# A Trainium2 backbone kernel: paired heads in the attention's values, summed filter weights, the inverses' block copies on other engines, and the products for L behind the DeltaNet preparation

## The chip, the core and the metric

The kernel runs on one core of a Trainium2 chip. The metric is the device time in microseconds of one execution, as the median of several runs. A core has TensorE (PE, matrix products, with PEld for its weight loads), VectorE (DVE), ScalarE (ACT), GpSimd (POOL) and SyncE (SP). In this kernel SyncE issues the transfers. Each engine takes its instructions in a fixed order.

## What is computed

One inference step of a hybrid backbone: two layers, width 1024, over 128 context tokens and 512 latent tokens, which the kernel holds side by side as 640 columns. Layer 0 is a half-step SwiGLU FFN, then RWKV-7 time mixing with 8 heads of 64 beside a gated DeltaNet with 4 heads of 128, then a second half-step FFN. Layer 1 has latent attention (8 heads) beside a Hyena convolution of order 2 in the same place. Every sub-layer is normalised and modulated by the condition.

The parts of the reference that the change meets:

```
def wkv7_scan(r, w, k, v, kk, a, S0):
    def step(S, xs):
        r_t, w_t, k_t, v_t, kk_t, a_t = xs
        sk = jnp.einsum('bhvk,bhk->bhv', S, kk_t)
        S = (S * w_t[:, :, None, :] - sk[..., None] * (kk_t * a_t)[:, :, None, :]
             + v_t[..., None] * k_t[:, :, None, :])
        return S, jnp.einsum('bhvk,bhk->bhv', S, r_t)
...
def gated_delta_chunked(q, k, v, g, beta, S0):
...
    T = lax.linalg.triangular_solve(eye + lower, jnp.broadcast_to(eye, lower.shape),
                                    left_side=True, lower=True, unit_diagonal=True)
...
def mla_attend(q_nope, q_pe, k_nope, k_pe, v):
...
        s = jnp.einsum('bqhd,bkhd->bhqk', qn, k_nope) + jnp.einsum('bqhr,bkr->bhqk', qp, k_pe)
        prob = jax.nn.softmax(s.astype(jnp.float32) * scale, axis=-1).astype(v.dtype)
        return jnp.einsum('bhqk,bkhd->bqhd', prob, v)
...
def hyena_filters(L, w1, b1, w2, b2, w3, freq):
...
    h = jnp.sin(freq[0] * (feats @ w1 + b1))
    h = jnp.sin(freq[1] * (h @ w2 + b2))
    h = (h @ w3).reshape(L, D_ORDER, 2, D_WIDTH)
...
    return h * window[:, None, None, :].astype(h.dtype)

def bidir_fftconv(z, h_f, h_b):
...
    filt2 = jnp.concatenate([h_f, jnp.zeros((1, C), h_f.dtype), h_b[:0:-1]], axis=0).astype(jnp.float32)
```

The final states and the compressed caches are returned besides the two outputs.

## The kernel before

Activations lie with channels on the 128 partitions and the 640 tokens along the free axis, in two halves of 320 columns. Large products are made of three: an activation and a weight are each split into a high and a low part (`hh` and `hl`, `wh` and `wl`), and high by high, low by high and high by low are summed in PSUM. The weights' split is a cast on ScalarE (`L470`, `L654`) and a subtraction on VectorE or GpSimd (`L471`, `L655`). All matmuls go through the helper `mm`, so most of TensorE's rows in the profile have its line, L287, and are told apart by the names of their tiles.

The order of instructions on each engine comes from the tile framework: it is given a program in the order of the Python code, simulates it with its own costs, and puts each engine's instructions in the order that this gives. An edit in one place can therefore move instructions in another. Pools with a number of buffers per name (`w` has 8, `PT` 2, `iv` 4) make a tile wait until the one that had its buffer is no longer read.

The stages, with their times in the profiled execution: the Hyena filters and the first modulations (0 to 93 us), the first FFN (to about 540), the input projection of layer 0 with the preparation of head pairs 0 and 1 (to about 895), the chunked scans with the preparation of pairs 2 and 3 (to about 1300), the output projection, two FFNs (to 2317), the latents (to 2390), the attention's heads with the Hyena convolution (to 2685), the output projection, and the last FFN from about 2750.

Four places matter here.

`filters()` makes the convolution filters. Two small layers with sines give features of 64 channels, doubled on both halves of the partitions; `hw3` holds the third layer's weights for both orders o and both directions d. For each order and each of five blocks of 128 tokens, two products (forward, backward) are multiplied by the window on VectorE (`fa`, `fb`), then GpSimd adds and subtracts them into `hpl` and `hmi`. For the first two blocks the backward filter's first token is zeroed (`nz`). Then `hpl` and `hmi` are transformed (`dfp`, `dfw`).

`rwkv_prep()` makes the scaled keys and queries of one pair of RWKV heads (tiles `w`, `kd`), and at its end the lower triangular blocks `L`: 40 products of 64 by 64 and four multiplications by a mask (L1116). Behind these comes the bonus term `b2`. `gdn_prep()` makes the same kind of blocks, `LT`, for one DeltaNet head. `prepare(i)` calls both, and then `inverses()`.

`inverses()` inverts 32 by 32 triangular blocks of both: they are stored to DRAM and loaded so that 120 blocks lie on 120 partitions (`iv`); 20 of them need a transpose, done by four strided copies on ScalarE (L1155). Then rows are eliminated one after the other (`invert_blocks`, L824 and L826), 8 of the 32 columns on GpSimd (`X0`), 24 on VectorE (`X8`). The results are stored, and four strided copies on ScalarE (L1168) make their transposes, which are stored too. Both come back with 28 loads or so on SyncE's queue (L1176 to L1182), and other stores and loads, those of the projection among them (`pd`, L871; `wr`, L469), stand in the same queue.

In the projection, a strip's PSUM is evicted into `pp` (L749 to L751), shifted against its neighbours (L881 with L882, or L911 with L912 and L913), put through an activation (L870) and stored to `pd`.

`heads()` runs over 8 heads and five blocks of 128 queries. `values()` transposes the probabilities into `PT`, and at a head's last block makes five products with `V` that write 64 rows of a PSUM bank: the lower rows for even heads, the upper for odd ones. ScalarE copies these into `om` (L1772), and after each odd head `om` is stored.

## Time and profile before

| | us |
|---|---|
| runs | 3216.09, 3218.57, 3236.96 |
| median of the runs | 3218.57 |
| profiled execution | 3213.42 |
| its span | 3211.6 |

The span is the time from the first to the last instruction of the profiled execution. The rows of the profile name a line, an engine, an operation, and the tiles written and read. In grouped rows the number behind the bar is busy time, then the mean duration in nanoseconds, then the idle time of the engine just before the group and what ended most of it. Stretches are given in microseconds from the span's start.

### The profile page before, as it was taken

The page shows a single profiled execution, that of the slowest core. Times are in us where ns is not written, and L with a number is a line of the kernel's source. Part 1 is how long each engine was busy: PE and PEld are TensorE (multiplying, and loading weights), DVE is VectorE, ACT ScalarE, POOL GpSimd, SP SyncE. Part 2 cuts the span into 40 slices and gives each one's busy share as a digit, 9 for nine tenths or more (in the row PEclk, how much of TensorE's full clock was granted, in tenths as well). Part 3 has the DMA queues.
Part 4 walks back from the last instruction along what each step waited for, and adds up shares of the span by engine and source line. Part 5 has one row for each costly group of instructions (what it writes and reads, how often), then busy time and mean ns, then how long its engine had stood idle before and what let it go on. Part 6 is the DMA issues. An engine that isn't in the chain of part 4 may idle for free.

```text
span 3211.6 us, 56035 instructions
## 1 busy us (share of the span) xinstructions
PE 2995.3 (93%) x21505; PEld 2680.3 (83%) x21505; DVE 2254.6 (70%) x3995; ACT 1375.1 (43%) x2876; POOL 1206.8 (38%) x1110
## 2 busy tenths in 40 slices
PE   7899999998789999889999979999999998899998
PEld 2799999987766666879999979999888747899998
DVE  5956667568678755695666797777865686877777
ACT  2523334566466644442333453333544423533333
POOL 4733334226425300273333474444310021644442
PEclk9999999999888988899999989999999999899999
DMA  7464542456465322445553222222421215222222
GB/s 267 148 205 162 180 135 72 168 167 170 126 155 128 84 75 66 144 145 187 170 172 121 83 93 90 84 79 83 128 61 51 85 50 180 66 86 82 87 83 82
DMA packets 277587, 385.36 MB, mean 120 GB/s; under 512 B 128704, under 2 KB 161120, under 8 KB 275400
## 3 DMA queue, kind: packets, MB, share of 16 engines
q1 hardware_dynamic: 277160, 381.13, 37.6%
q8 instruction: 169, 2.77, 0.3%
q14 instruction: 98, 0.80, 0.1%
q0 software_dynamic: 160, 0.66, 0.1%
HBM read 330.29 MB, written 51.42 MB: 119 GB/s over the span
## 4 chain that ended last, share of the span: by engine, by line
PE 53%; DVE 13%; DMA 4%; ACT 4%; issue 3%; POOL 1%; SPq 1%; DVEq 0%; ACTq 0%; POOLq 0%
PE ps L287 52%; DMA wr<-in_wd_dram 1%; DVE wl L655 1%; DMA wr<-in_wo_dram 1%; DVE nx L539 1%; DVE inv L824 1%; DVE wl L471 1%; DVE X L826 1%; DVE nacc L514 0%; PE ps L1765 0%; DMA pd<-o 0%; DVE b L605 0%; POOL X L826 0%; ACT wh L470 0%; DVE nx L710 0%
## 5 line engine op out<-in xcount | busy, mean ns | idle before, releaser
L287 PE MATMUL ps<-hh,wh 128*128 128x320 f32 x2208 | 694.7, 316 | 21.1 <-ACT pp L750 13.3
L287 PE MATMUL ps<-hl,wh 128*128 128x320 f32 x2208 | 690.2, 314 | 3.0 <-POOL hl L546 2.7
L287 PE MATMUL ps<-hh,wl 128*128 128x320 f32 x2208 | 681.1, 313 | 8.8 <-DVE wl L471 4.6
L287 PE MATMUL ps<-b,wh 128*128 128x320 f32 x2112 | 480.8, 315 | 36.0 <-DVE b L605 20.1
L287 PEld LDWEIGHTS ps<-hh,wh 128*128 128x128 f32 x2208 | 419.6, 190 | 36.4 <-ACT pp L750 13.6
L287 PEld LDWEIGHTS ps<-hh,wl 128*128 128x128 f32 x2208 | 417.3, 190 | 12.1 <-DVE wl L471 5.6
L287 PEld LDWEIGHTS ps<-hl,wh 128*128 128x128 f32 x2208 | 419.6, 190 | 7.3 <-POOL hl L546 3.9
L287 PEld LDWEIGHTS ps<-b,wh 128*128 128x128 f32 x2112 | 360.9, 192 | 43.9 <-DVE b L605 22.3
L287 PE MATMUL ps<-hidl,wh 128*128 128x320 f32 x1248 | 383.2, 309 | 0.0
L287 PE MATMUL ps<-hidh,wh 128*128 128x320 f32 x1248 | 382.6, 312 | 0.0
L287 PE MATMUL ps<-hidh,wl 128*128 128x320 f32 x1248 | 381.0, 309 | 0.9 <-DVE wl L471 0.9
L550 DVE SCALAR_TENSOR_TENSOR x<-ps,mod,x 128x128 f32<-128x128 f32 (+2 forms) x528 | 212.3, 434 | 215.7 <-PE ps L287 214.2
L655 POOL TENSOR_TENSOR wl<-S,wh 128x512 fp32r<-128x512 f32 x176 | 253.1, 1438 | 280.8 <-ACT wh L654 279.2
L684 POOL TENSOR_TENSOR S<-wr,wu 128x512 f32<-128x512 f32 x88 | 131.7, 1497 | 587.7 <-DMA wr<-in_wgu_dram 366.9
L287 PE MATMUL ps<-b,wl 128*128 128x320 f32 x1056 | 329.8, 314 | 10.4 <-DVE wl L655 7.8
L470 ACT CAST wh<-wr 128x512 fp32r<-128x512 f32 (+2 forms) x210 | 157.8, 754 | 394.0 <-PE ps L287 307.9
L654 ACT CAST wh<-S 128x512 fp32r<-128x512 f32 (+1 forms) x264 | 201.2, 764 | 241.8 <-PE ps L287 186.6
L471 DVE TENSOR_TENSOR wl<-wr,wh 128x512 fp32r<-128x512 f32 (+2 forms) x210 | 187.0, 893 | 86.2 <-ACT wh L470 84.2
L287 PEld LDWEIGHTS ps<-hidh,wh 128*128 128x128 f32 x1248 | 232.7, 188 | 13.2 <-issue 7.4
L287 PEld LDWEIGHTS ps<-hidh,wl 128*128 128x128 f32 x1248 | 233.3, 188 | 1.2 <-DVE wl L471 1.2
L287 PEld LDWEIGHTS ps<-hidl,wh 128*128 128x128 f32 x1248 | 233.9, 188 | 0.0
L287 PEld LDWEIGHTS ps<-b,wl 128*128 128x128 f32 x1056 | 202.2, 192 | 13.2 <-DVE wl L655 9.8
(455 smaller groups left out, 6047.9 us busy)
## 6 DMA issues: line engine op xcount, KB each, us to landing
wmod<-in_wmod_dram SPq DMA_DIRECT2D x288, 256.0 KB
wr<-in_wgu_dram SPq DMA_DIRECT2D x108, 512.0 KB
wu<-in_wgu_dram SPq DMA_DIRECT2D x88, 512.0 KB
wr<-in_wd_dram SPq DMA_DIRECT2D x80, 320.0 KB
wr<-in_wd_dram SPq DMA_DIRECT2D x96, 256.0 KB
pd<-o SPq DMA_DIRECT2D x32, 320.0 KB
wr<-in_abg_dram SPq DMA_DIRECT2D x17, 512.0 KB
wr<-in_wo_dram SPq DMA_DIRECT2D x16, 512.0 KB
```

The source lines that it names most:

```text
L287: self.nc.tensor.matmul(out=out, lhsT=lhsT, rhs=rhs, start=start, stop=stop)
L470: nc.scalar.copy(out=wh, in_=w)
L471: nc.vector.tensor_sub(out=wl, in0=w, in1=wh.bitcast(F32))
L539: nc.vector.scalar_tensor_tensor(out=xn[:, a:b], in0=self.x[c][:, k, a:b], scalar=A, in1=r[:, a:b], op0=ALU.mult, op1=ALU.mult)
L550: self.nc.vector.scalar_tensor_tensor(out=self.x[c][:, d, a:b], in0=q[:, a:b], scalar=gate[:, cond, d:d + 1], in1=self.x[c][:, d, a:b], op ...
L654: nc.scalar.copy(out=hi, in_=r)
L655: eng.tensor_tensor(out=lo, in0=r, in1=f32(hi), op=ALU.subtract)
L684: G.tensor_tensor(out=out, in0=x, in1=y, op=op)
L824: eng.tensor_tensor(out=tm, in0=L[s // 16][:, s % 16, t].unsqueeze(1).broadcast_to([np_, a, b]), in1=X[:, :a, s].unsqueeze(2).broadcast_to ...
L826: eng.tensor_tensor(out=X[:, :a, t], in0=X[:, :a, t], in1=tm, op=ALU.subtract)
```

## The change

Four edits:

1. In `values()`, nothing is multiplied at an even head's end. At an odd head's end ten products follow one another, the even head's and the odd head's in turn, into the lower and the upper 64 rows of one bank, and one copy of 128 rows evicts both.
2. In `filters()`, the forward and backward weights are replaced by their sum and their difference before the products, so that a product times the window is already `hpl` or `hmi`. The adds on GpSimd go. Where the backward filter's first token has to be zero, row 0 of both results is set to half of their sum. The blocks are taken in the order (0, 3), (1, 4), (2), in which neighbours read the lower and the upper 64 partitions.
3. In `inverses()`, the four transposing copies at the beginning go to GpSimd, and those at the end to the engine that made the columns: GpSimd for `X0`, VectorE for `X8`.
4. In `rwkv_prep()`, the products and masks for `L` are wrapped in `late()`, which `prepare()` calls behind `gdn_prep()`.

```diff
@@ -936,6 +936,7 @@
                 self.gdn_gates()
             self.mark(f"gA{i}")
             G[i] = self.gdn_prep(i, sets[i % 3])
+            R[i]["late"]()
             self.mark(f"J{i}")
             if i > 0:
                 next(inv[i - 1])
@@ -1100,21 +1101,23 @@
         for d, (kd, G) in enumerate(ks):
             nc.vector.tensor_mul(out=kd, in0=kd, in1=G)
             put(XD, d, d, kd)
-
-        at, _ = CONST["rmask"]
-        mask = self.const[:, at:at + CH].unsqueeze(1)
-        n = NCH // 2
-        for c0 in range(0, NCH, n):
-            qs = [self.ps("ma"), self.ps("ma")]
-            for i in range(n):
-                for d in range(2):
-                    for hh, q in enumerate(qs):
-                        hr = slice(64 * hh, 64 * hh + 64)
-                        self.mm(q[64 * d:64 * d + 64, CH * i:CH * i + CH], PQ[d][1][hr, c0 + i], PQ[d][0][hr, c0 + i])
-            for hh, q in enumerate(qs):
-                g = NCH * hh + c0
-                nc.vector.tensor_tensor(out=L[:, g:g + n], in0=q[:, :n * CH].rearrange("p (u m) -> p u m", u=n),
-                                        in1=mask.broadcast_to([P, n, CH]), op=ALU.mult)
+        def late():
+
+            at, _ = CONST["rmask"]
+            mask = self.const[:, at:at + CH].unsqueeze(1)
+            n = NCH // 2
+            for c0 in range(0, NCH, n):
+                qs = [self.ps("ma"), self.ps("ma")]
+                for i in range(n):
+                    for d in range(2):
+                        for hh, q in enumerate(qs):
+                            hr = slice(64 * hh, 64 * hh + 64)
+                            self.mm(q[64 * d:64 * d + 64, CH * i:CH * i + CH], PQ[d][1][hr, c0 + i], PQ[d][0][hr, c0 + i])
+                for hh, q in enumerate(qs):
+                    g = NCH * hh + c0
+                    nc.vector.tensor_tensor(out=L[:, g:g + n], in0=q[:, :n * CH].rearrange("p (u m) -> p u m", u=n),
+                                            in1=mask.broadcast_to([P, n, CH]), op=ALU.mult)
+
 
         nc.vector.scalar_tensor_tensor(out=kds, in0=kds, scalar=self.col("r_k", hp), in1=r, op0=ALU.mult, op1=ALU.mult)
         q = self.both(blk, kds, "ma")
@@ -1124,7 +1127,7 @@
             nc.vector.scalar_tensor_tensor(out=b2[:, cs], in0=q[c][:, :H], scalar=0.5, in1=v[:, cs], op0=ALU.mult, op1=ALU.mult)
         b2d = self.t(self.dp, [P, T], "b2", bufs=4)
         nc.sync.dma_start(out=b2d, in_=b2)
-        return dict(ZD=ZD, XD=XD, L=L, eG=eG, b2=b2d)
+        return dict(ZD=ZD, XD=XD, L=L, eG=eG, b2=b2d, late=late)
 
 
     def inverses(self, R, G):
@@ -1152,7 +1155,7 @@
             nc.sync.dma_start(out=raw[i], in_=dr[0][:g0, 16 * i:16 * i + 16])
         for i in range(2):
             for j in range(2):
-                nc.scalar.copy(out=L[i][:g0, :, 16 * j:16 * j + 16], in_=raw[j].rearrange("p t s -> p s t")[:, 16 * i:16 * i + 16])
+                nc.gpsimd.tensor_copy(out=L[i][:g0, :, 16 * j:16 * j + 16], in_=raw[j].rearrange("p t s -> p s t")[:, 16 * i:16 * i + 16])
         xs = []
         for j0, nj, eng in ((0, NPOOL, nc.gpsimd), (NPOOL, 32 - NPOOL, nc.vector)):
             X = self.t(ra, [nb, nj, 32], f"X{j0}")
@@ -1161,11 +1164,11 @@
             nc.gpsimd.memset(flat[:, j0::33], 1.0)
             self.invert_blocks(eng, L, X, j0, self.t(ra, [nb, 192], "inv", bufs=2))
             nc.sync.dma_start(out=dr[1][:, j0:j0 + nj], in_=X)
-            xs.append((X, j0))
+            xs.append((X, j0, eng))
         for i in range(2):
             xt = iv([nb, 16, 32])
-            for X, j0 in xs:
-                nc.scalar.copy(out=xt[:, :, j0:j0 + X.shape[1]], in_=X.rearrange("p s t -> p t s")[:, 16 * i:16 * i + 16])
+            for X, j0, eng in xs:
+                eng.tensor_copy(out=xt[:, :, j0:j0 + X.shape[1]], in_=X.rearrange("p s t -> p t s")[:, 16 * i:16 * i + 16])
             nc.sync.dma_start(out=dr[2][:, 16 * i:16 * i + 16], in_=xt)
         yield
 
@@ -1765,13 +1768,14 @@
                     nc.tensor.transpose(out=q[:, P * i:P * i + P], in_=pr[:, P * (g + i):P * (g + i) + P], identity=ident)
                 nc.vector.tensor_copy(out=PT[hh][:, g:g + n, P * (qi - 1):P * qi],
                                       in_=q[:, :P * n].rearrange("p (k t) -> p k t", k=n))
-            if qi == 4:
+            if qi == 4 and e == 1:
+
                 q = self.ps("tr")
                 for i in range(5):
-                    self.mm(q[rows], V[:, 1 + i, 64 * hh:64 * hh + 64], PT[hh][:, i], start=i == 0, stop=i == 4)
-                nc.scalar.copy(out=om[hh // 2][rows, P:], in_=q[rows])
-                if e == 1:
-                    nc.sync.dma_start(out=mix[hh // 2], in_=om[hh // 2])
+                    for g in (hh - 1, hh):
+                        self.mm(q[64 * (g % 2):64 * (g % 2) + 64], V[:, 1 + i, 64 * g:64 * g + 64], PT[g][:, i], start=i == 0, stop=i == 4)
+                nc.scalar.copy(out=om[hh // 2][:, P:], in_=q)
+                nc.sync.dma_start(out=mix[hh // 2], in_=om[hh // 2])
 
         units = [(hh, qi) for hh in range(8) for qi in range(5)]
         project(0)
@@ -1838,20 +1842,26 @@
         hb = self.t(fp, [P, 2, 512], "hbias")
         nc.sync.dma_start(out=hb, in_=I["hbias"].unsqueeze(0).broadcast_to([P, 2, 512]))
         for o in range(2):
+
+            w0, w1 = [W["hw3"][:, (2 * o + d) * 512:(2 * o + d) * 512 + 512] for d in range(2)]
+            nc.vector.tensor_tensor(out=w0, in0=w0, in1=w1, op=ALU.add)
+            nc.vector.scalar_tensor_tensor(out=w1, in0=w1, scalar=-2.0, in1=w0, op0=ALU.mult, op1=ALU.add)
             hpm = [self.t(fp, [P, 5, 512], n) for n in ("hpl", "hmi")]
-            for t in range(5):
-                q = [self.ps("mx"), self.ps("mx")]
-                for d in range(2):
-                    r, c = (slice(0, 64), t) if t < 3 else (slice(64, P), t - 3)
-                    self.mm(q[d], x[r, P * c:P * c + P], W["hw3"][r, (2 * o + d) * 512:(2 * o + d) * 512 + 512])
-                a, b = self.t(fp, [P, 512], "fa", bufs=2), self.t(fp, [P, 512], "fb", bufs=2)
-                nc.vector.tensor_tensor(out=a, in0=q[0], in1=W["win"][:, t], op=ALU.mult)
-                if t < 2:
-                    nc.vector.scalar_tensor_tensor(out=b, in0=q[1], scalar=self.con("nz"), in1=W["win"][:, t], op0=ALU.mult, op1=ALU.mult)
-                else:
-                    nc.vector.tensor_tensor(out=b, in0=q[1], in1=W["win"][:, t], op=ALU.mult)
-                nc.gpsimd.tensor_tensor(out=hpm[0][:, t], in0=a, in1=b, op=ALU.add)
-                nc.gpsimd.tensor_tensor(out=hpm[1][:, t], in0=a, in1=b, op=ALU.subtract)
+
+            for ts in ((0, 3), (1, 4), (2,)):
+                q = {(t, d): self.ps("mx") for t in ts for d in range(2)}
+                for d, w in enumerate((w0, w1)):
+                    for t in ts:
+                        r, c = (slice(0, 64), t) if t < 3 else (slice(64, P), t - 3)
+                        self.mm(q[t, d], x[r, P * c:P * c + P], w[r])
+                for t in ts:
+                    for d in range(2):
+                        nc.vector.tensor_tensor(out=hpm[d][:, t], in0=q[t, d], in1=W["win"][:, t], op=ALU.mult)
+                    if t < 2:
+                        a, b = hpm[0][0:1, t], hpm[1][0:1, t]
+                        nc.vector.tensor_tensor(out=a, in0=a, in1=b, op=ALU.add)
+                        nc.scalar.mul(out=a, in_=a, mul=0.5)
+                        nc.scalar.copy(out=b, in_=a)
                 yield
             bias = hb[:, o]
             for cs in range(2):
```

What this makes of the order, at three places. In these rows the number behind a name is the tile's, and the two programs count tiles apart.

TensorE at the end of the first head, before. `PT` are its probabilities, `ch` and `cl` the latents that the next heads' keys are made of:

```order
L287 MATMUL ps_26233<-hh_25346,wl_26228 128x320
L287 MATMUL ps_26311<-ch_25499,wh_26302 128x384
L287 MATMUL ps_26063<-PT_25961,V_25776 64x512 x5
L1912 MATMUL ps_26142<-const_58,cv_26135 128x128 x4
L287 MATMUL ps_26311<-cl_25500,wh_26302 128x384
L287 MATMUL ps_26311<-ch_25499,wl_26303 128x384
```

And at the first place of this kind after the change, at the end of the second head:

```order
L287 MATMUL ps_26697<-ql_25452,wh_26690 128x320
L287 MATMUL ps_26697<-qh_25451,wl_26691 128x320
L287 MATMUL ps_26451<-PT_25937,V_25752 64x512
L287 MATMUL ps_26451<-PT_26349,V_25752 64x512
L287 MATMUL ps_26451<-PT_25937,V_25752 64x512
L287 MATMUL ps_26451<-PT_26349,V_25752 64x512
```

The products stand at the end of every second head, and the rows of the first and the second head (`PT_25937`, `PT_26349`) take turns, ten in all; before, five of one head stood together.

ScalarE in the projection, where pair 1's inverses begin, before. `iv` and `zg` are blocks of pair 0's and pair 1's inverses, `o` the shifted strips, `wh` a weight's high part:

```order
L1195 ACTIVATE iv_8105<-ps_8107 32x320 x2
L1195 ACTIVATE iv_8105<-ps_8108 32x320 x2
L1201 ACTIVATE zg_8106<-ps_8109 128x160
L911 ACTIVATE o_8721<-pp_1193_6218,cols_59 128x128
L911 ACTIVATE o_8721<-pp_1193_6218,cols_59 128x512
L470 CAST wh_8996<-wr_8995 128x1024
L1155 COPY iv_8258<-iv_8262 20x16x16
L1155 COPY iv_8259<-iv_8262 20x16x16
L1155 COPY iv_8258<-iv_8263 20x16x16
L1155 COPY iv_8259<-iv_8263 20x16x16
L870 ACT_TABLE_LOAD
L870 ACTIVATE o_8721<-o_8721 128x640
```

And after (`o_8697` is what `o_8721` was):

```order
L911 ACTIVATE o_8697<-pp_1173_6194,cols_59 128x128
L911 ACTIVATE o_8697<-pp_1173_6194,cols_59 128x512
L1198 ACTIVATE iv_8081<-ps_8083 32x320 x2
L470 CAST wh_8972<-wr_8971 128x1024
L1198 ACTIVATE iv_8081<-ps_8084 32x320 x2
L1204 ACTIVATE zg_8082<-ps_8085 128x160
L870 ACTIVATE o_8697<-o_8697 128x640
L911 ACTIVATE o_8765<-pp_1172_6190,cols_59 128x128
```

The four copies of L1155 are gone from between L911 and L870 of one strip, and the evictions of pair 0's results (L1195, now L1198), which stood ahead of that strip, stand in this place.

TensorE at the products for pair 1's `L`, before. `w` are the scaled keys and queries, `hh`, `hl`, `wh` and `wl` a strip of the projection:

```order
L287 MATMUL ps_8537<-hh_6082,wh_8531 128x320
L287 MATMUL ps_8537<-hl_6083,wh_8531 128x320
L287 MATMUL ps_8537<-hh_6082,wl_8532 128x320
L287 MATMUL ps_7915<-w_7846,w_7847 64x64
L287 MATMUL ps_7916<-w_7846,w_7847 64x64
L287 MATMUL ps_7939<-w_7846,w_7847 64x64
L287 MATMUL ps_8537<-hh_6082,wh_8531 128x320
L287 MATMUL ps_8537<-hl_6083,wh_8531 128x320
```

And after, where `long` and `const` are the head sums of the bonus term (`wl_8575` is what `wl_8599` was, the strip that followed):

```order
L287 MATMUL ps_8579<-hh_5847,wl_8575 128x320
L287 MATMUL ps_8580<-hh_6058,wh_8574 128x320
L287 MATMUL ps_8580<-hl_6059,wh_8574 128x320
L287 MATMUL ps_8580<-hh_6058,wl_8575 128x320
L287 MATMUL ps_7892<-long_7795,const_58 128x320
L287 MATMUL ps_7893<-long_7795,const_58 128x320
L287 MATMUL ps_8013<-w_7822,w_7823 64x64
L287 MATMUL ps_8013<-w_7836,w_7837 64x64
```

The products stood within a strip; now the head sums stand ahead of them, and they come in the second half of the next strip.

## The prediction

> **What bounds the kernel now.** I read the page's head first, then the busy time by stage, then who waited for whom inside the stages that the change touches, and last the timeline where a wait is long.
>
> ```profile
> span 3211.6 us, 56035 instructions
> PE 2995.3 (93%) x21505; PEld 2680.3 (83%) x21505; DVE 2254.6 (70%) x3995; ACT 1375.1 (43%) x2876; POOL 1206.8 (38%) x1110
> PE 53%; DVE 13%; DMA 4%; ACT 4%; issue 3%; POOL 1%; SPq 1%; DVEq 0%; ACTq 0%; POOLq 0%
> ```
>
> TensorE is busy for 93% of the span, so all idle time together is 216 us, and matmul time saved is worth most where nothing else is full. The stages differ. The stretches are: the start (0 to 160), the first FFN (160 to 540), layer 0's projection with the preparation of head pairs 0 and 1 (540 to 895), the scans (895 to 1160), and the attention with the Hyena convolution (2390 to 2700). Columns are busy time and instruction count of each engine, granted clock, DMA share.
>
> ```profile
> 0.00:160.00 160.00, 125.15 (x614) 76.96 (x615) 117.53 (x152) 59.31 (x110) 93.77 (x67) 0.96 0.57 207
> 160.00:540.00 380.00, 380.00 (x2827) 356.46 (x2827) 246.39 (x405) 129.57 (x219) 149.73 (x106) 1.00 0.47 152
> 540.00:895.00 355.00, 308.09 (x2318) 293.96 (x2316) 233.67 (x406) 206.80 (x411) 143.59 (x229) 0.95 0.53 155
> 895.00:1160.00 265.00, 246.19 (x2903) 176.47 (x2904) 197.31 (x529) 168.88 (x514) 90.96 (x199) 0.91 0.47 120
> 2390.00:2700.00 310.00, 290.52 (x1426) 214.62 (x1425) 214.91 (x518) 112.00 (x309) 39.72 (x29) 0.97 0.23 77
> ```
>
> The reader is to see that the first FFN has no idle TensorE at all (380.00 of 380), so the few instructions there that change places cost nothing and bring nothing. The four edits lie in the other four stretches, with 35, 47, 19 and 19 us idle.
>
> **Paired heads.** The values products and their evictions, by form, and one head's five products (two records each) in the timeline; the last row is another product whose outputs are quarters of the columns, written alternately.
>
> ```profile
> L287 PE MATMUL ps<-PT,V 128*64 128x512 f32 x80 | 36.0, 597 | 0.7 <-DVE PT L1766 0.7
> L1772 ACT COPY om<-ps 64x512 f32<-64x512 f32 x8 | 4.6, 579 | 43.9 <-PE ps L287 43.9
> 2421.82 4.51 PE L287 MATMUL ps<-PT,V 128*64 128x512 f32 x10
> 24.12 1.07 PE L287 MATMUL ps<-wmod,cond 128*32 128x256 f32 x16
> L287 PE MATMUL ps<-wmod,cond x1152: 379/379/636, 17.4 to 1739.9; 128*32 128x256 f32 x192
> ```
>
> Each head now takes 4.51 us for 10 records, 0.45 us a record, 0.88 ns a column. The count of matmuls stays; neighbours now go to different halves of the columns. Do the halves run together? With quarters, 16 records take 1.07 us: the first needs its 0.379 us, so three more rounds of four take 0.23 us each, 0.90 ns a column for four at a time. That is the rate of a single one in the row above, so I take full overlap: a pair takes 4.5 us, eight groups become four, and TensorE loses 18.0 of 36.0 us. The bound below is nothing, if halves behave unlike quarters.
>
> A cost between the two: one record lasts 0.597 us (the first row's mean), a third longer than the 0.45 from one to the next. If a round had to end before the next began, ten rounds would take 5.97 us a pair and 23.9 in four, and 12.1 us would be saved. The Trainium skill, "TensorE: Matmul & The Clock Gate" (Part 3: Packing small matmuls), says that matmuls of different column groups overlap, and gives 2.38 times, not 3, for three of them; by that efficiency two halves would save 13.4 us here, an estimate from that page, and the quarters' row does not agree with so large a loss.
>
> How much of the 18.0 comes out at the end depends on who is full where these groups stand. Four of the eight stand between 2421 and 2541, for which the first row below speaks; the others stand later, for which the other two speak.
>
> ```profile
> 2500.00:2520.00 20.00, 20.00 (x110) 15.50 (x109) 10.44 (x31) 7.81 (x21) 1.80 (x1) 1.00 0.06 18
> 2560.00:2580.00 20.00, 19.74 (x57) 8.92 (x58) 19.89 (x47) 5.10 (x16) 3.15 (x3) 1.00 0.30 98
> 2580.00:2600.00 20.00, 16.91 (x73) 10.89 (x73) 19.80 (x43) 5.85 (x17) 7.37 (x5) 1.00 0.17 53
> ```
>
> For the first four heads TensorE is full and VectorE half idle: all 9 us count. For the last four VectorE is as full as TensorE, and I count 5 of 9 (the ends are 0 and 9; the last pair's group is followed only by its eviction and the output projection, so at least its share counts). Paired heads: **-14** (0 to -18). The wider evictions (four instead of eight) stand on an engine with over 15 us in 20 free. The probabilities of an even head stay in their buffer one head longer, with two buffers; the next head's first write stands behind the pair's product in TensorE's order anyway, so this costs nothing.
>
> **Summed filter weights.** Who computes what at the start, the two full stretches, and the first FFN's first product:
>
> ```profile
> L287 PE MATMUL ps<-hw,u 64*128 64x512 f32 x40 | 19.7, 627 | 0.0
> L1853 POOL TENSOR_TENSOR hpl<-fa,fb 128x512 f32<-128x512 f32 x10 | 12.9, 1291 | 43.9 <-DVE fb L1850 33.6 <-DVE fb L1852 10.1
> L1854 POOL TENSOR_TENSOR hmi<-fa,fb 128x512 f32<-128x512 f32 x10 | 14.0, 1402 | 0.0
> L1848 DVE TENSOR_TENSOR fa<-ps,win 128x512 f32<-128x512 f32 x10 | 6.9, 687 | 9.0 <-PE ps L287 7.9 <-POOL hmi L1854 1.0
> 13.30 0.68 DVE L1819 TENSOR_SCALAR u<-ps,cols 128x384 f32<-128x384 f32 x1 [2.23 <-PE ps L287]
> 60.00:80.00 20.00, 19.25 (x75) 6.68 (x74) 15.59 (x26) 5.69 (x15) 13.77 (x11) 1.00 0.14 53
> 80.00:100.00 20.00, 17.93 (x67) 11.42 (x67) 19.40 (x30) 9.99 (x25) 12.30 (x10) 0.91 0.47 171
> 93.45 0.71 PE L287 MATMUL ps<-hh,wh 128*128 128x320 f32 x1
> ```
>
> GpSimd loses 20 adds, 26.9 us. VectorE keeps 20 multiplies at 0.69 us, and gains four operations of 512 columns on the weights (about 4 x 0.7 = 2.8 us) and four one-row adds (at most 0.69 each). The four stand between the two sine layers, where VectorE sat idle for 2.23 us, so the second layer comes 0.6 us later, which the wait for the modulation weights behind it covers. Sixteen of the 20 matmuls now alternate between the upper and lower 64 rows; if those overlap, at most 0.8 x 19.7 / 2 = 7.9 us of TensorE go. Half of them stand in 60 to 80, where TensorE is full; after 80 VectorE is. Between product and filter transform the chain loses an add of 1.3 to 1.4 us. Start: **-2.5** (+2 if the weights arrive late, -6 if all overlap counts).
>
> **Inverses' copies, and the products for L behind the DeltaNet preparation.** These meet in the same stretch, so they are costed together. The waits of TensorE in 540 to 895, ScalarE around the longest, and what SyncE issued before it:
>
> ```profile
> PE ps L287 <- ACT pp L750: 13.3, 1, 13.3
> PE ps L287 <- DVE w L1094: 8.4, 2, 8.2
> 826.11 1.01 ACT L911 ACTIVATE o<-pp,cols 128x128 f32<-128x128 f32 x2 [4.42 <-DMA pd<-o]
> 831.18 1.18 ACT L1155 COPY iv<-iv 20x256 f32<-20x256 f32 x2 [1.77 <-DMA iv<-bl]
> 833.49 1.15 ACT L1155 COPY iv<-iv 20x256 f32<-20x256 f32 x2 [1.13 <-DMA iv<-bl]
> 835.94 0.74 ACT L870 ACTIVATE o<-o 128x640 f32<-128x640 f32 x1
> 843.74 0.30 ACT L750 COPY pp<-ps 128x192 f32<-128x192 f32 x1
> 800.47 4.14 SPq L1163 DMA_DIRECT2D bl<-X  x2
> 822.59 1.44 SPq L871 DMA_DIRECT2D pd<-o  x1
> L1155 ACT COPY iv<-iv 20x256 f32<-20x256 f32 x16 | 9.2, 632 | 11.4 <-DMA iv<-bl 11.4
> L1059 POOL COPY w<-long 128x640 f32<-128x640 f32 x4 | 2.9, 725 | 8.2 <-DMA long<-pd 8.2
> L1438 POOL COPY rS<-rs 64x5 f32<-64x5 f32 x2 | 0.5, 264 | 0.0
> L1766 DVE COPY PT<-ps x64: 273/482/692, 2404.1 to 2678.9; 128x512 f32<-128x512 f32 x32, 128x128 f32<-128x128 f32 x32
> 760.00:780.00 20.00, 11.84 (x117) 11.08 (x116) 19.93 (x23) 15.67 (x31) 18.42 (x14) 0.83 0.49 144
> 960.00:980.00 20.00, 16.07 (x137) 10.79 (x137) 19.66 (x34) 18.16 (x43) 14.01 (x13) 0.83 0.31 90
> L1094 DVE TENSOR_TENSOR w<-w,w x8: 804/817/2191, 688.3 to 981.4; 128x640 f32<-128x640 f32 x8
> ```
>
> The 13.3 us end with L750. Between L911 and L870 ScalarE stood in two waits for block loads and four copies, 1.77 + 1.18 + 1.13 + 1.15 = 5.2 us, and L870's store feeds the rest of the chain. With the copies on GpSimd this goes; the changed order puts two pairs of evictions there instead, each bounded by L911's pair of 1.01 us. I take 4.5 us off the 13.3 (3.2 if those cost their bound, 8 if the waits behind L870 go too). The start of this chain does not move: the store at 822.59 still stands on SyncE behind X's stores and the loads that follow them, and X ends with GpSimd's share.
>
> That share gets longer by six copies an inverse, four of 20x256 and two of 120x128. GpSimd's price for such a copy is not in the trace; its ends are 0.26 and 0.73 us (L1438, L1059), and I take 0.45, 2.7 us an inverse. VectorE gets two of 120x384, between 0.27 and 0.69 us (L1766), 1 us an inverse. The four of 20x256 take the place of ScalarE's four (4 x 0.63 = 2.5 us) in the chain, so what is new on it is 3.7 - 2.5, about +1 each for pairs 0 and 1. In the scans ScalarE is nearly full (18.16 of 20 in 960 to 980), and four copies of 0.63 us leave it beside the chunk chain's evictions; I count 1 of the 2.5 us: -1 for each of pairs 2 and 3.
>
> The 8.2 us wait for L1094 goes as such, since the 40 products that needed it now stand behind projection strips. But VectorE is full there (19.93 of 20 in 760 to 780), and the next strip's split weights come from VectorE too, in nearly the same place of its order. What is late next is that split, so most of the 8.2 us returns a strip later: -2 (0 to -8). The stores of L leave SyncE later, behind the gates' loads; the inverse needs the DeltaNet blocks as well and starts no later. Together: -4.5 + 2 - 2 - 2 = **-6.5** (+12 to -16).
>
> The sum: -14 - 2.5 - 6.5 = -23. The profiled execution took 3213.4 us (span 3211.6 and 1.8 around it), which becomes 3190.4. The median of the runs, 3218.57, lies 5.2 above the profiled one, so I add about 2 for a profile in the middle of its runs: **3192 us**, 0.8% under the median.
>
> **Rivals.**
> 1. *More is released.* Both preparation waits vanish (-13.3 - 8.2), the start gives its 6, and paired heads give 18: 3213.4 - 45.5 = 3168. For it: 47 us idle in that stretch; against it: VectorE full in 760 to 780, and SyncE's row of issues from 800 to 822.59, which no edit shortens.
> 2. *The halves do not run together, or in part.* If not, paired heads give 0, and the time is 3192 + 14 = 3206. If each round of two has to end first, they give 14 x 12.1 / 18 = 9.4, and the time is 3196.6. The quarters' row speaks against both, and for the second that it is not of halves. The Trainium skill, "TensorE: Matmul & The Clock Gate" (Part 3), would make of it 14 x 13.4 / 18 = 10.4, an estimate of 3195.6.
> 3. *Slower: VectorE and GpSimd hold each other up in the inverses.* Rows for one operation spread from 0.82 to 2.19 us (L1094), so a copy on one engine can cost the other 1.4 us. With six GpSimd copies an inverse, all on the chain, that is 8.4 us an inverse, 33.6 in four, and the gains of 6.5 go too: 3213.4 - 16.5 + 33.6 = 3230. It decides from 16.5 / 4 = 4.1 us an inverse upward. The Trainium skill, "SBUF — State Buffer" (Who interferes with whom), says that a VectorE instruction with two SBUF inputs contends with GpSimd's reads while ScalarE waits on nobody, which speaks against moving copies off ScalarE; the spread of L1094 agrees with it. Against this rival: the six copies last 2.7 us by my price, less than the 4.1 from which it decides, unless each holds up the other engine for longer than itself.
>
> **How the numbers follow.** Forecast 0.60 (3178 to 3204), more released 0.15, no overlap 0.08, overlap in part 0.07, slower chain 0.10. The range from 3168 to 3214 leaves out the slower chain and half of rival 1, under two in ten. A difference under 1%, 32 us, can hardly be told from no change: faster by over 1% means under 3186.4, which takes rival 1 and a good third of the forecast, 0.36; slower by over 1% means over 3250.8, beyond rival 3's price, 0.04; within 1% is 0.60.
>
> **What would show it.** In the changed profile: four groups of 20 values records at 4.5 us each, busy 18 (not 36); 2390 to 2700 shorter by 14; no adds on GpSimd before 80 and the first FFN's product 2 to 3 us earlier than 93; the wait for L750 near 8; GpSimd's copies at 0.3 to 0.6 us. I am wrong if the values records still sum to 36 us, if the wait for L750 stays or grows, or if the scans get longer.

## The result and the profile after

The changed kernel took 3190.67 us, median of four runs (3187.27 to 3194.21). Four runs of the kernel before on the same chip had a median of 3223.64. The ratio is 0.9908, with a 95% interval of 0.9883 to 0.9932: faster by 0.9%. The profiled execution took 3187.27 us, 26.2 less than the one of before. The head of its page (span, busy time of each engine, and each engine's share of the chain of work that ended last), and then the busy time of three of the stages:

```profile
span 3184.8 us, 56026 instructions
PE 2972.9 (93%) x21505; PEld 2678.8 (84%) x21505; DVE 2259.5 (71%) x4011; ACT 1359.8 (43%) x2846; POOL 1195.1 (38%) x1114
PE 55%; DVE 10%; DMA 4%; ACT 3%; issue 3%; POOL 2%; SPq 1%; DVEq 0%; ACTq 0%; POOLq 0%
```

```profile
0.00:160.00 160.00, 125.09 (x613) 77.28 (x613) 118.71 (x160) 63.89 (x117) 68.34 (x48) 0.93 0.58 206
895.00:1160.00 265.00, 242.22 (x2848) 174.00 (x2849) 198.95 (x540) 160.42 (x502) 97.23 (x211) 0.91 0.48 122
2390.00:2700.00 310.00, 287.29 (x1542) 226.03 (x1541) 230.41 (x524) 118.21 (x311) 42.91 (x32) 0.97 0.29 96
```

TensorE lost 22.4 us of busy time and its share stayed 93%. GpSimd's 20 adds at the start are gone (93.77 to 68.34 busy). Fixed windows hold other work once things move, so from here on stretches are cut at the work itself: the **projection** from the end of the first FFN's products to the end of layer 0's projection, the **scans** from there to that layer's output projection, the **attention** from its first scores to its output projection. In these windows the columns are as in the prediction: length, busy time and count of TensorE, weight load, VectorE, ScalarE and GpSimd, granted clock, DMA share and GB/s. The three stretches before:

```profile
577.60:889.00 311.40, 269.23 (x2062) 256.39 (x2062) 203.87 (x345) 183.60 (x366) 136.25 (x222) 0.95 0.53 157
889.00:1294.90 405.90, 369.23 (x3993) 261.37 (x3992) 274.02 (x758) 229.55 (x713) 95.92 (x208) 0.88 0.37 99
2392.20:2687.80 295.60, 277.26 (x1357) 202.59 (x1356) 206.63 (x504) 106.36 (x299) 38.16 (x28) 0.98 0.20 67
```

And after:

```profile
577.80:889.60 311.80, 278.37 (x2063) 264.34 (x2062) 206.69 (x349) 172.12 (x347) 140.47 (x231) 0.93 0.52 153
889.60:1284.50 394.90, 354.85 (x3993) 254.07 (x3991) 272.44 (x762) 221.43 (x698) 103.29 (x223) 0.90 0.40 105
2379.70:2661.30 281.60, 259.31 (x1358) 197.51 (x1356) 212.43 (x505) 104.47 (x295) 39.13 (x28) 0.97 0.21 70
```

The attention is 14.0 us shorter, the scans 11.0, the projection 0.4 longer. The start up to the first FFN's second strip is 0.2 longer (178.9 to 179.1). That leaves 2.4 us of the span's 26.8 for all the rest. The scans need care: the counts are those of before, and length times granted clock is 357 before and 355 after (405.9 x 0.88, 394.9 x 0.90). Nearly the same work ran at a higher clock.

### The profile page after: what moved, and what is told of

The parts are those of the page before. It is cut to its first block, busy times and chain, and to the rows that moved or that the text cites. A ratio compares the mean times of both kernels' runs of the same rounds, so it can differ in the third digit from the quotient of the medians.

```text
span 3184.8 us, 56026 instructions
## 1 busy us (share of the span) xinstructions
PE 2972.9 (93%) x21505; PEld 2678.8 (84%) x21505; DVE 2259.5 (71%) x4011; ACT 1359.8 (43%) x2846; POOL 1195.1 (38%) x1114
## 4 chain that ended last, share of the span: by engine, by line
PE 55%; DVE 10%; DMA 4%; ACT 3%; issue 3%; POOL 2%; SPq 1%; DVEq 0%; ACTq 0%; POOLq 0%
PE ps L287 54%; DMA wr<-in_wd_dram 1%; DVE wl L655 1%; POOL S L684 1%; DMA wr<-in_wo_dram 1%; DVE nx L539 1%; DMA pd<-o 1%; POOL wl L655 1%; DVE wl L471 1%; DVE nacc L514 0%; PE ps L1768 0%; ACT wh L470 0%; DVE b L605 0%; PE ps L1284 0%; DVE X L826 0%
```

## The experiments

Ratios are against runs of the kernel before on the same chip, 3 or 5 rounds each. Lengths are from one profiled execution each, in us; the second strip is that of the first FFN; "clock" is that of the scans.

| kernel | ratio, 95% interval | 2nd strip begins | projection | scans, clock | attention |
|---|---|---|---|---|---|
| before | | 178.9 | 311.4 | 405.9, 0.88 | 295.6 |
| whole change | 0.9908 (0.9883 to 0.9932) | 179.1 | 311.8 | 394.9, 0.90 | 281.6 |
| whole, again | 0.9907 (0.9877 to 0.9936) | 179.3 | 310.9 | 389.1, 0.92 | 281.4 |
| paired heads alone | 0.9965 (0.9943 to 0.9988) | 181.4 | 310.4 | 417.2, 0.86 | 283.2 |
| summed weights alone | 0.9977 (0.9958 to 0.9996) | 180.3 | 311.6 | 398.7, 0.92 | 296.9 |
| copies alone | 0.9973 (0.9946 to 1.0000) | 184.6 | 302.7 | 417.3, 0.85 | 296.8 |
| products for L alone | 1.0009 (0.9990 to 1.0028) | 179.6 | 309.2 | 406.5, 0.88 | 296.5 |
| without products for L | 0.9931 (0.9910 to 0.9951) | 179.6 | 303.3 | 405.7, 0.88 | 281.0 |
| the same, one more profile | none | 179.7 | 303.0 | 422.6, 0.83 | 281.1 |
| without copies | 0.9947 (0.9926 to 0.9968) | 179.3 | 311.8 | 397.3, 0.89 | 282.2 |
| without summed weights | 0.9940 (0.9918 to 0.9963) | 179.1 | 311.8 | 402.7, 0.90 | 283.2 |
| heads in turn | 0.9957 (0.9934 to 0.9979) | 178.8 | 314.1 | 391.8, 0.91 | 291.9 |
| late only for pairs 2, 3 | 0.9947 (0.9926 to 0.9968) | 177.9 | 303.9 | 421.2, 0.85 | 281.7 |
| late only for pairs 0, 1 | 0.9935 (0.9914 to 0.9955) | 181.9 | 311.0 | 393.7, 0.90 | 283.4 |

No version beats the whole change. The four edits alone sum to -0.76%, against -0.92% for all together: within the intervals they add up, though the stretches, as will be seen, do not.

### The paired heads

The first kernel has this edit of the diff alone.

```diff
-            if qi == 4:
+            if qi == 4 and e == 1:
...
+                    for g in (hh - 1, hh):
+                        self.mm(q[64 * (g % 2):64 * (g % 2) + 64], V[:, 1 + i, 64 * g:64 * g + 64], PT[g][:, i], start=i == 0, stop=i == 4)
```

> Only the paired heads; everything else as before. Theory (the change's gain has two places, 14 us in the attention and 11 us in the scans, and the attention's share is the paired heads' alone): the attention stretch, from its first query-key product to the output projection's first, shortens from 295.6 to about 282 us, the values' busy time is 18.0 us, and the scans stay at 405.9 us between the last projection product and the output projection; about 14 us faster (-0.43%). Rival (the order that the framework makes moves work in other stages as well): the scans or the FFNs move by more than 3 us.

The attention fell to 283.2 and the values products to 18.0 us busy, so the saving there belongs to this edit. All that TensorE has to do ahead of the first values product stands in the same order as before, and yet the scans took 417.2 us, not 405.9. Their length thus varies from one execution to the next with no edit in them.

The second kernel keeps the pair in one group but writes one head's five products after the other's.

```diff
-                for i in range(5):
-                    for g in (hh - 1, hh):
+                for g in (hh - 1, hh):
+                    for i in range(5):
```

> The whole change, but at an odd head's end the five products of the even head come first and then the five of the odd one. Theory 1 (the gain needs neighbours in different halves of the columns): the values' busy time is about 33 us or more again instead of 18.0, and the attention's stretch about 294 us instead of 281.6; 12 to 14 us slower than the whole change. Theory 2 (the gain comes from having four groups and four evictions instead of eight, or from the new places in the order): the stretch stays within 4 us of 281.6.

One group in the timeline and all four in the groups, first of the whole change, then of this kernel:

```profile
2445.59 4.51 PE L287 MATMUL ps<-PT,V 128*64 128x512 f32 x20
L287 PE MATMUL ps<-PT,V 128*64 128x512 f32 x80 | 18.0, 597 | 0.7 <-DVE PT L1769 0.7
```

```profile
2443.69 7.14 PE L287 MATMUL ps<-PT,V 128*64 128x512 f32 x20
L287 PE MATMUL ps<-PT,V 128*64 128x512 f32 x80 | 28.6, 597 | 0.7 <-DVE PT L1769 0.7
```

The same 20 records take 4.51 us with the heads alternating and 7.14 in turn, and the attention is 10.3 us longer, close to the 10.6 between the busy times. So the full gain needs neighbours in different halves; the merged group and the wider eviction without them leave 3.7 of the 14.0 us. In turn still beats 9.02 us, two heads apart: the second head's first record starts beside the first head's seventh of ten, about four ahead of its turn. That is why it came out below what was expected.

### The start

This edit alone, whose hunk in the diff is that of the filters:

```diff
+            nc.vector.tensor_tensor(out=w0, in0=w0, in1=w1, op=ALU.add)
+            nc.vector.scalar_tensor_tensor(out=w1, in0=w1, scalar=-2.0, in1=w0, op0=ALU.mult, op1=ALU.add)
...
-                nc.gpsimd.tensor_tensor(out=hpm[0][:, t], in0=a, in1=b, op=ALU.add)
-                nc.gpsimd.tensor_tensor(out=hpm[1][:, t], in0=a, in1=b, op=ALU.subtract)
```

> Only the summed filter weights. Theory (what the start gains is given back before the first FFN's first strip is done, since another supply sets that): the filter transforms end about 6 us earlier than before (88 instead of 94 us), but the first FFN's second strip begins where it did, 179 us, within 0.5, and the time is the same within 3 us. Rival (the start's gain counts): 2 to 5 us faster, all of it ahead of 179 us.

The filter transforms ended at 87.7 instead of 94.0 us, and the second strip began no earlier. The end of the start in the whole change (window, timeline, and the longest of TensorE's waits there, columns: total, times, longest) shows why:

```profile
80.00:95.00 15.00, 7.87 (x18) 3.18 (x18) 14.29 (x20) 7.60 (x17) 9.89 (x7) 0.91 0.32 123
84.73 3.60 PE L287 MATMUL ps<-hmi,dfw 128*128 128x512 f32 x8
95.41 0.64 PE L287 MATMUL ps<-hh,wh 128*128 128x320 f32 x1 [7.09 <-DVE g L1891]
PE ps L287 <- DVE g L1891: 7.1, 1, 7.1
```

And the same window before:

```profile
80.00:95.00 15.00, 12.93 (x32) 6.42 (x33) 14.40 (x25) 8.25 (x21) 9.01 (x9) 0.89 0.36 140
```

VectorE is busy for over 14 of 15 us in both. TensorE is through 6 us earlier and then waits 7.1 us for VectorE's last operation on the transformed filters (L1891). The first FFN's first product starts at 95.41 us where it had started at 93.45, so it comes 2 us later instead of earlier: VectorE was the limit and its work did not shrink. By the second strip the two kernels are level again; what sets that place was not singled out. The whole change with the filters as before:

```diff
-            nc.vector.tensor_tensor(out=w0, in0=w0, in1=w1, op=ALU.add)
...
+                nc.gpsimd.tensor_tensor(out=hpm[0][:, t], in0=a, in1=b, op=ALU.add)
+                nc.gpsimd.tensor_tensor(out=hpm[1][:, t], in0=a, in1=b, op=ALU.subtract)
```

> The change without its second edit: the filters as before, with GpSimd's adds. Theory 1 (VectorE is the limit between the filters and the first FFN, so the edit brings nothing): the first FFN's second strip begins at 179 to 185 us as in all runs, and the time is that of the whole change within 4 us. Theory 2 (the edit's 7 us in the timed run of it alone are its own): 5 to 9 us slower than the whole change.

Its second strip also begins at 179.1. Timed, the edit shows 0.23% alone, an interval that barely excludes nothing, and 0.3% by leaving it out, where the intervals overlap. In the profile of the edit alone the 7 us stand in the scans, which took 398.7 us at a clock of 0.92 instead of 405.9 at 0.88. All ten timed runs of that kernel have a granted clock of 0.962 to 0.965 over the whole execution, which 5 of the 31 runs of the kernel before reach. So this gain goes with the clock; whether the edit brings that clock is not shown.

### The copies and the products for L

The copies alone, of the blocks of L and of X:

```diff
-                nc.scalar.copy(out=L[i][:g0, :, 16 * j:16 * j + 16], in_=raw[j].rearrange("p t s -> p s t")[:, 16 * i:16 * i + 16])
+                nc.gpsimd.tensor_copy(out=L[i][:g0, :, 16 * j:16 * j + 16], in_=raw[j].rearrange("p t s -> p s t")[:, 16 * i:16 * i + 16])
...
-                nc.scalar.copy(out=xt[:, :, j0:j0 + X.shape[1]], in_=X.rearrange("p s t -> p t s")[:, 16 * i:16 * i + 16])
+                eng.tensor_copy(out=xt[:, :, j0:j0 + X.shape[1]], in_=X.rearrange("p s t -> p t s")[:, 16 * i:16 * i + 16])
```

> Only the inverses' copies moved from ScalarE to GpSimd and VectorE. Theory 1 (ScalarE's copies stood beside the chunk chain's evictions, and their going is the scans' gain): the scans shorten from 405.9 us to about 395, and the preparation's wait for L750 falls from 13.3 to under 9 us. Theory 2 (the scans' gain comes from the place of the products for L): scans within 3 us of 405.9. Theory 3 (VectorE and GpSimd hold each other up): the projection stretch or the scans get longer by 5 us or more.

And the products for L alone, with their masked evictions in the new function:

```diff
+            R[i]["late"]()
...
+        def late():
```

> Only the products for L moved behind the DeltaNet preparation. Theory 1 (as in the run with the copies alone): the 8.2 us wait of TensorE for L1094 goes, but returns as waits a strip later, so the last projection product stays at 889 us within 3 and the scans within 3 us of 405.9. Theory 2 (the scans' gain comes from here): the scans shorten by 8 us or more. Theory 3 (the later products are late for the inverses): the scans get longer.

Waits of TensorE between 540 and 895 that differ. Two of before, beside the 13.3 us for L750 and the 8.4 us for L1094 that the prediction shows:

```profile
PE ps L1459 <- ACT ps L1471: 3.2, 2, 2.4
PE ps L1400 <- DVE long L1392: 1.3, 1, 1.3
```

With the copies alone:

```profile
PE ps L287 <- DVE L L1116: 5.9, 2, 4.7
PE ps L287 <- DVE w L1094: 5.4, 2, 5.1
PE ps L287 <- DMA gn<-bl: 5.0, 1, 5.0
PE ps L287 <- ACT pp L750: 1.4, 1, 1.4
```

With the products for L alone (lines are three higher below the edit):

```profile
PE ps L287 <- ACT pp L750: 12.7, 1, 12.7
PE ps L1462 <- ACT ps L1474: 8.1, 2, 6.0
PE ps L1403 <- DVE long L1395: 3.2, 1, 3.2
```

And in the whole change:

```profile
PE ps L1462 <- ACT ps L1474: 7.1, 2, 5.1
PE ps L1403 <- DVE long L1395: 3.2, 1, 3.2
PE ps L287 <- ACT pp L750: 2.8, 1, 2.8
PE ps L287 <- DVE w L1127: 2.5, 1, 2.5
```

The copies take the wait for L750 from 13.3 to 1.4 us and 8.7 off the projection. How, is seen in SyncE's queue with the copies alone, at X's last store and the next two stores of strips:

```profile
814.67 0.35 SPq L1163 DMA_DIRECT2D bl<-X  x1
815.12 0.33 SPq L871 DMA_DIRECT2D pd<-o  x1
833.68 0.39 SPq L871 DMA_DIRECT2D pd<-o  x1
```

The first strip's store goes out right behind X and ahead of the blocks' loads. Before, it stood behind these loads, at 822.59, and the second followed at 836.71. So the new order of this queue seems to have a part in the 8.7 us, beside the copies that left ScalarE; no run changed it alone.

The moved products end the wait for L1094, and in its place the waits for L1474 and L1395 (L1471 and L1392 before) grow from 4.5 us to 10 or 11. Alone, the move took 2.2 us off the projection and left the scans within 1 us. The copies alone had scans of 417.3 us, which the third theory would claim, but at a clock of 0.85 length times clock is 355: again the clock. Is it the combination that costs the 8.7 again? The next two leave one of the two edits out of the whole change, first the move, with the products for L back in the preparation:

```diff
-            R[i]["late"]()
...
-        def late():
```

> The change without its fourth edit: the products for L stand where they stood before. Theory 1 (the two edits in the preparation undo one another: the later products put TensorE behind the DeltaNet head's waits, and this eats what the copies gave): the stretch from the first FFN's end to the last projection product is 302 to 305 us instead of 311.8, and the kernel is 6 to 9 us faster than the whole change, about 1.1% under the kernel before. Theory 2 (with all edits the stretch is limited by something else, so the fourth edit costs nothing there): 310 to 312 us, and the time is that of the whole change within 3 us.

Then the copies, those of L and those of X:

```diff
-                nc.gpsimd.tensor_copy(out=L[i][:g0, :, 16 * j:16 * j + 16], in_=raw[j].rearrange("p t s -> p s t")[:, 16 * i:16 * i + 16])
+                nc.scalar.copy(out=L[i][:g0, :, 16 * j:16 * j + 16], in_=raw[j].rearrange("p t s -> p s t")[:, 16 * i:16 * i + 16])
...
-                eng.tensor_copy(out=xt[:, :, j0:j0 + X.shape[1]], in_=X.rearrange("p s t -> p t s")[:, 16 * i:16 * i + 16])
+                nc.scalar.copy(out=xt[:, :, j0:j0 + X.shape[1]], in_=X.rearrange("p s t -> p t s")[:, 16 * i:16 * i + 16])
```

> The change without its third edit: the inverses' copies stay on ScalarE. Theory 1 (the scans are shorter only where the copies are off ScalarE and the products for L of pairs 0 and 1 come late, as in the five programs that have both, 389 to 403 us): projection 309 to 311 us, scans 403 to 420 us, about 0.6% under the kernel before. Theory 2 (the late products alone do it): scans 388 to 398, about 0.9% under. In both, length times granted clock of the scans is 357 within 6, and the attention 281 to 283.

The projection answered plainly: 303.3 without the moved products, 311.8 without the copies. The first theory also wanted the kernel without the moved products to be faster than the whole change, and it wasn't: its scans took 405.7 us. Without the copies the scans took 397.3 us, as the second theory had it, but the time fell by 0.5% and not 0.9. So I ran the whole change a second time, without an edit, and then split the move by pairs (pairs 0 and 1 are prepared in the projection, 2 and 3 in the scans).

> The whole change once more, the program unchanged. Theory 1 (the 11 us that the scans were shorter in the first profile are the granted clock of that execution and no effect of the change): the scans' stretch comes out anywhere from 394 to 417 us, with length times granted clock near 357 as in every run so far, while the projection (311.8), the attention (281.6) and the FFNs repeat within 1 us. Theory 2 (the change shortens the scans): the scans repeat at 395 within 3 us.

Neither theory was met to the letter: the scans took 389.1 us, shorter than both had it, at a clock of 0.92. Late only for pairs 2 and 3:

```diff
-            R[i]["late"]()
+            if i >= 2:
+                R[i]["late"]()
...
+        if hp < 2:
+            late()
```

> The whole change, but the products for L stand behind the DeltaNet preparation only for head pairs 2 and 3; for pairs 0 and 1, which are prepared beside the projection, they stand where they stood. Theory 1 (the fourth edit costs 8 us in the projection by pairs 0 and 1 and gives 10 to 15 in the scans by pairs 2 and 3, so both can be had): first FFN's end to last projection product 303 us, scans 388 to 396, about 3176 us, 1.2 to 1.3% under the kernel before and 6 to 8 us under the whole change. Theory 2 (the scans' gain comes from pair 1's place, or is chance): projection 303, scans 403 to 417, the time that of the change without the fourth edit.

The last has `i < 2` and `hp >= 2` in those two places, so only pairs 0 and 1 come late.

> The converse: late only for pairs 0 and 1. Theory 1: projection 311 us, scans 403 to 417, the slowest of these, about 3203 us. Theory 2: projection 311, scans 388 to 396, the time that of the whole change.

The projection follows one rule in all fourteen profiles: 302.7 to 303.9 with the copies and early products for pairs 0 and 1 (four), 309.2 to 314.1 wherever those products are late (seven), 310.4 to 311.6 with neither edit (three). The split goes with SyncE's queue: in the four the first strip's store stands ahead of the blocks' loads, in the other ten behind them. What was saved there by one half of this change was spent by the other. But late for pairs 2 and 3 alone, which kept the 303.9, had scans of 421.2 us, and no gain came of it. The converse had scans of 393.7 us and was timed the same within the intervals (0.9935 against 0.9947).

One more profile of the kernel without the moved products asked whether its scans repeat.

> The change without its fourth edit once more, for the profile. Theory 1 (this program's scans keep falling to half clock in the middle, at about 90 us from the stretch's start): scans 403 us or more with at least one stretch of over 15 us at half clock between 80 and 300 us, length times clock near 357. Theory 2 (half-clock stretches come by chance in any of these programs): under 398 us without one.

They did not repeat: 422.6 us after 405.7, of which a stretch of 47.8 us at half clock. Two windows of it:

```profile
1150.00:1200.00 50.00, 48.48 (x462) 33.92 (x462) 18.45 (x55) 14.93 (x46) 0.00 (x0) 0.52 0.18 45
1200.00:1220.00 20.00, 19.77 (x202) 14.29 (x203) 12.79 (x38) 11.59 (x41) 0.39 (x1) 1.00 0.26 77
```

This longest stretch stood 270 us into the scans, not near 90 us, though two of 13.7 us stood at 96 and 113; by length the reading of a varying clock holds, by place only in part. Over all fourteen profiles the scans average 396.6 us where the products for pairs 0 and 1 are late (seven) and 412.7 where they are early (seven), and length times clock averages 357 and 358. So the difference goes with the granted clock. Whether the late products bring the better clock, or seven against seven was luck, is open: the two groups overlap (389.1 to 406.5, 398.7 to 422.6), and the timed split by pairs, above, shows no such gain.

## Why the prediction came out right, and which of its terms did not

The forecast was 3192.0 us and the time 3190.67; the sum was -23 from the profiled execution, which fell by 26.2. The terms were less good than the sum.

- **Paired heads, -14: right.** 14.0 in the whole change, 14.2 in its repeat, 12.4 alone. The groups take 4.51 us, 18.0 in four, as full overlap said, so rival 2 fell: two halves gave 2.00 times (9.02 to 4.51), not the efficiency of 2.38 in three that the Trainium skill, "TensorE: Matmul & The Clock Gate" (Part 3: Packing small matmuls), states for groups of 32 columns. For halves the measurement decides.
- **Start, -2.5: wrong, +0.2.** The failed step is "Between product and filter transform the chain loses an add of 1.3 to 1.4 us", counted although VectorE is the full engine after 80. TensorE did lose its time: the products with `hw` went from 19.7 to 16.2 us busy, and the transforms ended 6 us earlier. The first FFN's first product came 2.0 us later, not 2 to 3 earlier. The row of VectorE at 19.40 of 20 had already spoken against the step.
- **Products for L, -2: right alone (2.2), wrong in sign beside the copies.** That the wait would return later was in the prediction, "a strip later" and as the split of weights. It returned in the chunk preparation (L1462, L1403) and not at the split, and with the copies it cost 8.5 us more than staying put (303.3 against 311.8). The projection without the moved products, to set beside that of the whole change:

```profile
578.40:881.70 303.30, 272.90 (x2064) 259.56 (x2063) 205.79 (x349) 175.34 (x350) 137.21 (x220) 0.94 0.53 158
```

Of the 8.5 us, 5.5 are TensorE's busy time (278.37 against 272.90) and 3.0 its idle time. Products on tile `w` are 2.9 of the 5.5 (10.92 against 8.00 us in these windows): more of the two heads' products for L, in different halves of the rows, were put one head after the other. What the rest is was not singled out; the granted clock is 0.93 against 0.94. All 320 products for L, of all four pairs, before, then after:

```profile
L287 PE MATMUL ps<-w,w 64*64 64x64 f32 x320 | 12.6, 241 | 12.5 <-DVE w L1094 10.5 <-DVE L L1116 2.0
```

```profile
L287 PE MATMUL ps<-w,w 64*64 64x64 f32 x320 | 17.7, 245 | 2.6 <-DVE w L1127 2.5
```

- **Copies, -4.5 and +2: the mechanism right in part, the net too small alone and gone in the whole.** Alone they gave 8.7, with one strip's store ahead of the blocks' loads, which the working did not have. In the whole change both strips' stores stand behind the loads, and the failed step is "start of this chain does not move". ScalarE's part of it, and what SyncE issued:

```profile
831.52 1.02 ACT L911 ACTIVATE o<-pp,cols 128x128 f32<-128x128 f32 x2 [12.39 <-DMA pd<-o]
836.37 0.73 ACT L870 ACTIVATE o<-o 128x640 f32<-128x640 f32 x1
845.46 0.30 ACT L750 COPY pp<-ps 128x192 f32<-128x192 f32 x1
816.24 0.33 SPq L1166 DMA_DIRECT2D bl<-X  x1
829.00 0.38 SPq L871 DMA_DIRECT2D pd<-o  x1
```

From L911 to L750 the chain is 13.9 us instead of 17.6, but L911 starts 5.4 us later. X's last store went out at 816.24, where SyncE was done with X by 804.6 before, and the strip's store stands behind it and the loads, 829.00 instead of 822.59. TensorE itself came later too: it reached the product that waits for L750 265.2 us into the stretch and waited 2.8 us, where it had been there after 253.2 us and waited 13.3; without the moved products it was there after 260.9 and waited 0.2. So this chain holds up at most 2.8 of the 8.5 us; the larger part, 4.3 by this point, is TensorE's own later arrival. GpSimd's share of X ended later, with other work between its steps in the changed order, and its copies last longer than I took:

```profile
L1158 POOL COPY iv<-iv 20x256 f32<-20x256 f32 x16 | 9.4, 622 | 76.2 <-DMA iv<-bl 76.2
L1171 POOL COPY iv<-X 120x128 f32<-120x128 f32 x8 | 3.5, 432 | 0.2
L1171 DVE COPY iv<-X 120x384 f32<-120x384 f32 x8 | 4.3, 542 | 0.1
```

Four at 0.62, two at 0.43 and two at 0.54 make 4.4 us an inverse; the working had 3.7 (0.45 each on GpSimd). Rival 3 didn't happen: its bound was 4.1 us an inverse for GpSimd's part, which is 3.35.

- **Scans, -2: the profile says -11, but not as work.** Counts are equal and ScalarE lost 8.1 us there as foreseen; all but about 2 of the 11 us go with the clock (length times clock 357 and 355), and 2 is what its rounding allows. This term, mis-sized by 9 us, made up for the 2.7 missing at the start and the 4.9 in the projection (-4.5 forecast, +0.4 measured). That is luck: in profiles of one unchanged program the scans differed by 5.8 us (394.9 and 389.1) and by 16.9 (405.7 and 422.6).

Rival 1 (3168) asked that VectorE and SyncE's queue let everything out; at both places they didn't. For the whole the forecast was right by its largest term, which was understood, and by luck in the smaller ones, whose errors had both signs.

## What to carry to other kernels

Narrow outputs of two independent groups, in different column halves and alternating in the order, cost half on TensorE here; the alternation gave most of it. Before counting a shorter chain as time, look for the engine that is full in the same window, and for the queue through which the result has to leave; and try edits that share a queue together, since alone each may show what the pair takes back. Where a stretch is made of small matmuls, compare length times granted clock before crediting an edit with its length.

## What was not expected of the hardware

In the scans TensorE ran at half its clock for long stretches. At the ends this is alike in all fourteen profiles: the mean granted clock is 0.66 to 0.79 in the first 40 us and 0.54 to 0.69 in the last 40. Between them, from 115 us after the start to 70 us before the end, it differs: 1.00 in three profiles, 0.87 in two, and the stretches stand in other places, some of them where TensorE is never idle. The same 20 us in the kernel with the paired heads alone and in the whole change:

```profile
1160.00:1180.00 20.00, 20.00 (x276) 14.83 (x276) 6.36 (x20) 5.27 (x16) 0.00 (x0) 0.50 0.22 61
```

```profile
1160.00:1180.00 20.00, 19.58 (x372) 14.84 (x372) 12.73 (x39) 9.88 (x32) 0.00 (x0) 1.00 0.24 64
```

The first is busy for all 20 us and granted 0.50; with 276 products instead of 372 it falls behind for as long as this lasts (34.1 us there, 47.8 in the longest). The Trainium skill, "TensorE: Matmul & The Clock Gate" (Part 1, What's actually happening), has activity release the throttle; by that a busy TensorE would be back at full clock soon, which these rows do not show for a stretch of small products (32x32 to 128x128). What sets it off was not found.

The second surprise is the reach ahead: products in the other half of the columns started about four records before their turn (7.14 us instead of 9.02 with the heads in turn), no more, so TensorE didn't make up for a poor order by itself.
